# A retrieval feed-forward layer: one of five dense token blocks keeps its dense first product, but fetches its chosen values and gathers rows of the second table

## The chip, the cores and the metric

The kernel runs on one core of one Trainium2 chip. The metric is the device time of one execution in microseconds (us). TensorE is called PE, VectorE DVE, ScalarE ACT and GpSimd POOL, as in the profile; SP is the engine that issues most of the ordinary DMAs, PEld the weight loads of PE. Each engine takes its instructions in the order in which the program lists them.

## The reference

One layer with 1024 tokens of width 1024: a mixer (a gated linear recurrence and a state-space group, both behind one input projection), then a feed-forward layer with product-key retrieval over 128 x 128 = 16384 experts, and a last norm. The change is in the retrieval layer:

```python
q = (xb @ wq).reshape(TOK_BLOCK, 8, 256)            # 8 heads
s1 = einsum('thd,kd->thk', q[..., :128], k1)        # 128 keys each
s2 = einsum('thd,kd->thk', q[..., 128:], k2)
v1, i1 = top_k(s1, 16); v2, i2 = top_k(s2, 16)
sc, cidx = top_k(all sums v1 + v2, 16)              # 16 experts a head
e = i1[cidx // 16] * 128 + i2[cidx % 16]
g = softmax(sc)
act = gelu(einsum('thkd,td->thk', u_tab[e], xb))    # first product
out = einsum('thk,thkd->td', g * act, v_tab[e])     # second product
```

So each token picks 8 x 16 = 128 experts. An expert is one row of u_tab (the first table) and one row of v_tab (the second), 1024 float32 numbers, 4 KB each.

## The kernel before, in words

The tokens lie in 8 blocks of 128. After the mixer (`front`) the retrieval layer (`peer`, L848) does the blocks in two ways.

**Gathered blocks** (the last NG = 3). `topk` (L982) finds the experts, `topk_gather` (L1067) writes their indices. `gather` (L1150) fetches, for k = 0 to 127, the k-th chosen row of the first table for all 128 tokens with one indirect DMA on POOL (`fetch`, L1130: 128 rows of 4 KB, 512 KB) and multiplies it with the tokens on DVE (tile `jkb`), which gives one column of `act`. After the gelu and the product with the gate weights `gw`, `act` is transposed on PE, and 128 indirect DMAs fetch rows of the second table, which PE sums up four at a time (tile `pgb`). A ring of ROWS = 7 buffers (`row`) holds the rows, with six fetches ahead. `finish` (L1197) does the last norm and stores the block.

**Dense blocks** (the first ND = 5, 640 tokens). The first product is made for all 16384 experts. For each of 128 slices j (`first`, L1217): load and split a 512 KB slice of the first table (tiles `ur`, `uh`, `ul`: float32 numbers as a sum of two shorter ones), 48 matmuls in two halves of 320 columns (tile `ap`), gelu on ACT. `build_g` (L1080) spreads a block's 128 gate weights per token over a matrix of all experts by products of one-hots (tiles `ohA`, `ohB`, `gp`, `gs`), which goes to DRAM as `G_d`. In `dense` (L1296) come 32 chunks of JC = 4 slices j: load the gate matrix (`gt`), multiply the first product by it (`hr` or `ha`), split it (`hh`, `hl`), load and split four slices of the second table (`vr`, `vh`, `vl`), and multiply: for each block 24 matmuls of 512 columns into a PSUM tile (`vp`, two buffers), which DVE adds to the block's result (`h`, L1363).

**What sets the order.** `Merge` (L62) is a planner: the parts are generators, and at each `yield` the one with the lowest clock goes on. The clocks come from costs that `Timed` (L121) charges for each compute instruction; a DMA is only charged where `mg.dma` and `mg.at` say so, and `Timed` hands DMA starts through without a charge (L128). The result is a fixed order of instructions for each engine. The stages are:

1. The norm and the queries of the gathered blocks, then (L1274) the queries of the dense blocks, the top-k of the gathered blocks and the start of the gathers.
2. The build stage (L1284): for each dense block the top-k and its gate matrix (`build`, L1278), and beside it first products made ahead (`ahead`, L1238), stored to DRAM as `A_d`. The order of j takes one slice of each chunk in turn, NA = 112 at most; 84 get done. Gathers go on, no closer than `pace` = 5.0 us of the planner's clock.
3. The dense stage (L1381): the 32 chunks. Of the 128 slices, 84 come back from `A_d`, the 44 late ones are made between the chunks, spread over all of them. Here the gathers are let through by `share`: a budget of DMA bytes that grows with PE's planned time (`step`, L1375) minus the bytes that the dense work loads.

SP issues the loads and the stores of `G_d` and `A_d`, POOL the indirect DMAs. Matmuls and most DVE and ACT instructions go through a helper, so that they all bear L146; in the profile they are told apart by their tiles.

Of the kernel before, what the change touches and what calls it, by code (L numbers as in the profile page):

```python
# [18 lines left out]
P = 128  # L19
D = 1024  # L20
# [815 lines left out]
ND = 5  # L836
NG = 8 - ND
TD = ND * P
HALF = TD // 2
TG = NG * P  # L840
JC = 4
NA = 112
# [5 lines left out]
def peer(tc, a, cst, pools, h, ss, mg):  # L848


    nc = tc.nc
# [4 lines left out]
    gblocks, dblocks = list(range(ND, 8)), list(range(ND))  # L856
# [4 lines left out]
    H_d = dr.tile([NG, P, D], F32, name="H_d")  # L861
# [4 lines left out]
    xDh = pc.tile([P, 8, TD], F32R, name="xDh")  # L866
    xDl = pc.tile([P, 8, TD], F32R, name="xDl")
    idx = [pc.tile([P, P], I32, name=f"idx{b}") for b in range(NG)]
    idxT = [pc.tile([P, P], I32, name=f"idxT{b}") for b in range(NG)]
    gw = [pc.tile([P, P], F32, name=f"gw{b}") for b in range(NG)]  # L870
# [4 lines left out]
    V.tensor_copy(i16, iota[:, 0:16])  # L875

# [24 lines left out]
    def norm2():  # L901
        for blocks in (gblocks, dblocks):
# [3 lines left out]
            for b in blocks:  # L906
# [69 lines left out]
    rows = pools.open("rows", bufs=ROWS)  # L976
    gp = pools.open("gp", bufs=2)
# [89 lines left out]
    def topk_gather(b):  # L1067
        i1, i2, g = yield from topk(b)
        n = b - ND
        V.scalar_tensor_tensor(i1, i1, 128.0, i2, ALU.mult, ALU.add)  # L1070
        V.tensor_copy(idx[n], i1)
# [77 lines left out]

    def gather(n):  # L1150
        xg = gp.tile([P, D], F32, name="xg", tag="xg", bufs=1)
        nc.sync.dma_start(xg, X_d[n])
        act = gp.tile([P, P], F32, name="act", tag="act", bufs=1)
        k = 0
        for ub in stream(a["peer_u"], [idx[n][:, k:k + 1] for k in range(P)]):
            yield gate()
            jk = gp.tile([P, D], BF, name="jkb", tag="jkb", bufs=1)
            V.tensor_tensor_reduce(jk, ub, xg, 1.0, 0.0, ALU.mult, ALU.add, act[:, k:k + 1])
            k += 1
            mg.units += 1  # L1160
        S.activation(act, act, AF.Gelu_apprx_tanh)
        yield
# [67 lines left out]

    order = [c * JC + jj for jj in range(JC) for c in range(P // JC)]
# [34 lines left out]
    def topks():  # L1266
        for n in range(NG):
            yield from topk_gather(ND + n)

    def dense_query():  # L1270
        yield from query(pqb, dblocks, xDh, xDl)
# [19 lines left out]
    pv = pools.open("pv", "right", bufs=4)  # L1291
    phh = pools.open("phh", "right", bufs=4)
    pgg = pools.open("pgg", "right", bufs=1)
    nch = P // JC

    def dense():  # L1296
        late = [[] for _ in range(nch + 1)]
        order[made[0]:] = sorted(order[made[0]:], key=lambda j: j // JC)
        for j in order[made[0]:]:
            late[j // JC].append(j)  # L1300
        ha = {}

        def products(js):
            for j in js:
                fetch_u()
# [158 lines left out]
```

## Time and profile before

| | |
|---|---|
| median of 3 runs | 3043.96 us (3030.63 to 3053.36) |
| profiled execution, its own time | 3037.66 us |
| its span | 3035.9 us |
| mean granted TensorE clock | 0.961 of full speed |
| HBM read, written | 664.75 MB, 85.20 MB |
| DMA, mean over the span | 248 GB/s |
| mixer and first norm | 0 to about 400 us |
| queries, first top-k | about 400 to 720 us |
| build stage | about 720 to 1593 us |
| dense stage | about 1593 to 3036 us |

How the lines are read. A row of a stretch gives from:to, its length, the busy time of each engine with the number of instructions, the granted TensorE clock (1.0 is full speed), the mean busy share of the 16 DMA engines, and GB/s. A row of a group gives line, engine, operation, out<-in, shapes and count, then busy time and mean duration in ns, then the idle time of the engine ahead of them and what ended it. Busy time of a group is a union: overlapping instructions count once, which is why count times mean duration of matmuls is more than the busy time. Float32 matmuls that are not split show up as two records. A few per cent of the matmul records are missing. A row of the waits gives who waited for whom, the sum in us, how often, and the longest. A row of the chain gives start, length and what ran there. A DMA row gives the count, the size of one and the median us from issue to landing.

### The profile page before, as it was taken

The numbers are of one execution on the slowest core, as the hardware profiler recorded it, in microseconds if no ns is written. First come the engines' busy times: TensorE is split into PE (matmuls) and PEld (weight loads), VectorE is DVE, ScalarE is ACT, GpSimd is POOL, SyncE is SP. The second block draws the span as 40 slices with busy tenths as digits, with TensorE's granted clock in tenths as the row PEclk, the third lists the DMA queues.
The fourth block names the chain that finished last, engine by engine and source line by source line (L and its number), as shares of the span: only waits on it lengthen the run. The fifth ranks groups of instructions, "written<-read, shape, count | busy, mean of one in ns | idle before, by whom it ended". The sixth has DMA issues, their size and how long they took to land.

```text
span 3035.9 us, 43516 instructions
## 1 busy us (share of the span) xinstructions
PE 2783.9 (92%) x16261; PEld 2352.3 (77%) x16261; DVE 2029.8 (67%) x4241; ACT 1155.0 (38%) x2273; POOL 955.2 (31%) x778
## 2 busy tenths in 40 slices
PE   6887999987999999999989999999999999999998
PEld 6765878877899988888877777676768788767675
DVE  7786452999999994332349999644547999643434
ACT  5355433321684958584852222211222212121212
POOL 0000000132526012222244555343435556343431
PEclk9988999988999999999999999999999999999999
DMA  4112144565989658888899889877878899787774
GB/s 156 28 26 100 42 138 128 181 223 197 309 305 350 217 193 289 277 277 290 274 327 343 328 325 322 304 251 285 323 293 305 319 342 344 268 303 260 257 275 160
DMA packets 298532, 754.01 MB, mean 248 GB/s; under 512 B 28368, under 2 KB 125840, under 8 KB 293200
## 3 DMA queue, kind: packets, MB, share of 16 engines
q0 software_dynamic: 110592, 402.70, 37.3%
q1 hardware_dynamic: 180992, 337.33, 31.8%
q10 hardware_dynamic: 6736, 11.19, 1.1%
q8 instruction: 128, 2.10, 0.3%
q14 instruction: 84, 0.69, 0.1%
HBM read 664.75 MB, written 85.20 MB: 247 GB/s over the span
## 4 chain that ended last, share of the span: by engine, by line
PE 36%; DVE 11%; DMA 9%; issue 7%; ACT 1%; POOL 1%; DVEq 0%; POOLq 0%; ACTq 0%
PE vp L146 14%; PE ap L146 13%; PE pgb L146 6%; DVE jkb L146 5%; PE gp L146 3%; DMA row<-in_peer_v_dram,idxT 3%; DMA ur<-in_uT_dram 2%; DVE h L146 2%; DVE vl L146 2%; DMA gt<-G_d 2%; DMA hr<-A_d 1%; DVE hl L146 1%; DMA A_d<-aa 1%; DVE hr L146 1%; POOL row L1132 1%
## 5 line engine op out<-in xcount | busy, mean ns | idle before, releaser
L1132 POOL DMA_INDIRECT row<-in_peer_u_dram,idx x384 | 525.2, 1368 | 772.8 <-DVE act L146 335.8
L1132 POOL DMA_INDIRECT row<-in_peer_v_dram,idxT x384 | 426.2, 1110 | 921.7 <-PE pgb L146 794.8
L146 PE MATMUL ap<-xDl,uh 128*128 128x320 f32 x2048 | 657.0, 321 | 25.9 <-ACT ha L146 21.4
L146 PE MATMUL ap<-xDh,ul 128*128 128x320 f32 x2048 | 644.4, 315 | 6.1 <-DVE ul L146 6.1
L146 PE MATMUL ap<-xDh,uh 128*128 128x320 f32 x2048 | 642.0, 314 | 0.0
L146 PE MATMUL vp<-vl,hh 128*128 128x512 f32 x1280 | 510.0, 400 | 39.6 <-DVE vl L146 29.4
L146 PE MATMUL vp<-vh,hl 128*128 128x512 f32 x1280 | 504.4, 394 | 0.7 <-DVE hl L146 0.7
L146 PE MATMUL vp<-vh,hh 128*128 128x512 f32 x1280 | 502.5, 393 | 0.0
L146 DVE CUSTOM_DVE_ANT_0 jkb<-row,xg 128x1024 bf16<-128x1024 f32 x384 | 468.4, 1220 | 10.9 <-DMA row<-in_peer_u_dram,idx 8.1
L146 PEld LDWEIGHTS ap<-xDl,uh 128*128 128x128 f32 x2048 | 392.7, 192 | 67.5 <-issue 29.3
L146 PEld LDWEIGHTS ap<-xDh,ul 128*128 128x128 f32 x2048 | 392.7, 192 | 9.1 <-DVE ul L146 7.4
L146 PEld LDWEIGHTS ap<-xDh,uh 128*128 128x128 f32 x2048 | 392.4, 192 | 1.3
L146 PEld LDWEIGHTS vp<-vl,hh 128*128 128x128 f32 x1280 | 242.0, 190 | 134.1 <-issue 27.5
L146 DVE TENSOR_TENSOR h<-h,vp 128x1024 f32<-128x1024 f32 x160 | 194.6, 1216 | 190.7 <-PE vp L146 190.7
L146 ACT ACTIVATE hh<-ha 128x640 fp32r<-128x640 f32 x44 | 32.3, 735 | 659.4 <-PE vp L146 654.8
L146 PEld LDWEIGHTS vp<-vh,hh 128*128 128x128 f32 x1280 | 242.5, 189 | 51.7
L146 PEld LDWEIGHTS vp<-vh,hl 128*128 128x128 f32 x1280 | 242.8, 190 | 50.9 <-DVE hl L146 2.7
L146 DVE TENSOR_TENSOR ul<-ur,uh 128x1024 fp32r<-128x1024 f32 x128 | 156.5, 1222 | 137.1 <-ACT uh L146 137.0
L146 PE MATMUL pgb<-row,W 128*32 128x512 f32 x1536 | 204.0, 608 | 24.9 <-DMA row<-in_peer_v_dram,idxT 24.9
L146 DVE TENSOR_TENSOR ohA<-iota,kt 128x512 f32<-128x512 f32 x160 | 110.2, 689 | 166.5 <-PE gp L146 166.3
L146 PE MATMUL gp<-ohB,ohA 128*128 128x128 f32 x1280 | 185.2, 282 | 22.7 <-DVE ohB L146 12.9
L146 ACT ACTIVATE ohB<-ohB,kt 128x128 f32<-128x128 f32 x480 | 203.9, 489 | 0.0
(422 smaller groups left out, 4194.6 us busy)
## 6 DMA issues: line engine op xcount, KB each, us to landing
ur<-in_uT_dram SPq DMA_DIRECT2D x128, 512.0 KB, 5.8
vr<-in_peer_v_dram SPq DMA_DIRECT2D x128, 512.0 KB, 6.8
G_d<-gs SPq DMA_DIRECT2D x20, 2048.0 KB, 11.7
gt<-G_d SPq DMA_DIRECT2D x32, 1280.0 KB, 8.6
A_d<-aa SPq DMA_DIRECT2D x84, 320.0 KB, 5.8
hr<-A_d SPq DMA_DIRECT2D x84, 320.0 KB, 7.1
wqr<-in_wq_dram SPq DMA_DIRECT2D x32, 512.0 KB, 4.0
S_d<-sc SPq DMA_DIRECT2D x64, 128.0 KB, 4.0
```

The costliest lines, as they stand in the source:

```text
L146: return fn(*args, **kw)
L1132: G.indirect_dma_start(out=r, out_offset=None, in_=table, in_offset=bass.IndirectOffsetOnAxis(ap=col, axis=0))
```

## The change

ND becomes 4, and a third kind of block comes in: NE = 1 block whose first product is still made densely, with the four others (NU = ND + NE = 5 blocks, TU = 640 columns), and whose second product is gathered.

- `first` and the queries work on the same 640 columns as before. After the first product of slice j, the 512 columns of the dense blocks go on as before, and the 128 columns of the fifth block are stored to DRAM in `E_d` (`chosen_only`, 64 KB a slice). After the last slice the planner's flag "U" is set.
- `values` fetches the fifth block's chosen values: 128 indirect DMAs on POOL, each of one number for each of 128 tokens, from `E_d` into the columns of `act`. Nothing in it moves the planner's clock. Then `act` is multiplied by `gw`, transposed, and rows of the second table are gathered as for the other gathered blocks.
- The gathers take blocks 6 to 8 first and the fifth last, after "U".
- Only four gate matrices are built. The fifth block's top-k comes after them, ahead of flag "g".
- First products are made ahead in the order of j (no NA), until "g" and then to the end of a chunk. The dense stage begins with the chunks whose first product is late and ends with those made ahead; each chunk is prepared while the second product of the one before is done. The parts of `dense` are written anew for that, and a tile `gt` has its buffer in the pool `phh`.
- The pace of the gathers in the build stage goes from 5.0 to 2.4 us, and the planned costs of a first and a second product are set to 7.0 and 2.7 us (6.5 and 2.6 before).

The diff, cut to its core:

```diff
-ND = 5
-NG = 8 - ND
+ND = 4
+NE = 1
+NU = ND + NE
+NG = 8 - NU
+NR = NE + NG
 TD = ND * P
-HALF = TD // 2
+TE = NE * P
+TU = NU * P
+HALF = TU // 2
 TG = NG * P
 JC = 4
-NA = 112
...
-    gblocks, dblocks = list(range(ND, 8)), list(range(ND))
+    gblocks, ublocks, dblocks = list(range(NU, 8)), list(range(NU)), list(range(ND))
...
-    H_d = dr.tile([NG, P, D], F32, name="H_d")
+    H_d = dr.tile([NR, P, D], F32, name="H_d")
+    E_d = dr.tile([P, P, TE], F32, name="E_d")
...
+    rows = pools.open("rows", bufs=ROWS)
+    gp = pools.open("gp", bufs=2)
+    pxu = pools.open("pxu")
+    xDh = pxu.tile([P, 8, TU], F32R, name="xDh")
+    xDl = pxu.tile([P, 8, TU], F32R, name="xDl")
...
-        for blocks in (gblocks, dblocks):
+        for blocks in (gblocks, ublocks):
...
-                    nc.sync.dma_start(X_d[b - ND], xn)
                     nc.sync.dma_start(H_d[b - ND], h[b])
-                    dh, dl, t0 = xGh, xGl, (b - ND) * P
+                if b >= NU:
+                    nc.sync.dma_start(X_d[b - NU], xn)
+                    dh, dl, t0 = xGh, xGl, (b - NU) * P
...
+        if n < NE:
+            at = pk.tile([P, P], F32, name="at", tag="rf")
+            V.scalar_tensor_tensor(at, i2, 128.0, i1, ALU.mult, ALU.add)
+            V.tensor_scalar(at, at, float(TE), tok[:, n:n + 1], ALU.mult, ALU.add)
+            V.tensor_copy(idx[n], at)
...
+        if n >= NE:
+            V.tensor_copy(idx[n], i1)
...
+    def values(n):
+        act = gp.tile([P, P], F32, name="ace", tag="ace")
+        flat = E_d.rearrange("j i t -> (j i t)").unsqueeze(1)
+        for k in range(P):
+            G.indirect_dma_start(out=act[:, k:k + 1], out_offset=None, in_=flat,
+                                 in_offset=bass.IndirectOffsetOnAxis(ap=idx[n][:, k:k + 1], axis=0))
+            if k % 8 == 7:
+                yield
+        return act
     def gather(n):
-        xg = gp.tile([P, D], F32, name="xg", tag="xg", bufs=1)
-        nc.sync.dma_start(xg, X_d[n])
-        act = gp.tile([P, P], F32, name="act", tag="act", bufs=1)
-        k = 0
-        for ub in stream(a["peer_u"], [idx[n][:, k:k + 1] for k in range(P)]):
-            yield gate()
-            jk = gp.tile([P, D], BF, name="jkb", tag="jkb", bufs=1)
-            V.tensor_tensor_reduce(jk, ub, xg, 1.0, 0.0, ALU.mult, ALU.add, act[:, k:k + 1])
-            k += 1
-            mg.units += 1
-        S.activation(act, act, AF.Gelu_apprx_tanh)
-        yield
+        if n < NE:
+            act = yield from values(n)
+        else:
+            xg = gp.tile([P, D], F32, name="xg", tag="xg", bufs=1)
...
+            S.activation(act, act, AF.Gelu_apprx_tanh)
+            yield
         V.tensor_tensor(act, act, gw[n], ALU.mult)
...
     def fetch_u(end=P):
         if len(nextu) < 2 and made[0] + len(nextu) < end:
-            nextu.append(load_split(pu, a["uT"][order[made[0] + len(nextu)]], [8, P], "u"))
+            nextu.append(load_split(pu, a["uT"][made[0] + len(nextu)], [8, P], "u"))
+    def chosen_only(j, t):
+        nc.sync.dma_start(E_d[j], t[:, TD:])
+        mg.dma(TE // 2)
+        if j == P - 1:
+            mg.flag("U")
     def ahead():
         fetch_u()
         yield
         while nextu:
-            t = pk2.tile([P, TD], F32, name="aa", tag="aa")
-            j = order[made[0]]
+            t = pk2.tile([P, TU], F32, name="aa", tag="aa")
+            j = made[0]
             for n, _ in enumerate(first(t, nextu[0])):
-                if n == 0 and "g" not in mg.flags:
-                    fetch_u(NA)
-                yield
-            nc.sync.dma_start(A_d[j], t)
-            mg.dma(320)
+                if n == 0:
+                    fetch_u(P if "g" not in mg.flags else JC * -(-(j + 1) // JC))
+                yield
+            nc.sync.dma_start(A_d[j], t[:, :TD])
+            mg.dma(TD // 2)
+            chosen_only(j, t)
             made[0] += 1
             nextu.pop(0)
...
-        for n in range(NG):
+        for n in list(range(NE, NR)) + list(range(NE)):
             if f"g{n}" not in mg.flags:
                 yield f"g{n}"
+            if n < NE and "U" not in mg.flags:
+                yield "U"
             yield from gather(n)
...
+        for n in range(NE, NR):
             yield from topk_gather(ND + n)
...
+        yield from query(pqb, ublocks, xDh, xDl)
...
         for b in dblocks:
             yield from build_g(b)
+        for n in range(NE):
+            yield from topk_gather(ND + n)
         mg.flag("g")
-    pace[0] = 5.0
+    pace[0] = 2.4
...
+    pv = pools.open("pv", "right", bufs=JC)
+    phh = pools.open("phh", "right", bufs=JC)
+    nch, nah = P // JC, made[0] // JC
...
+        def prepare(c):
+            gt = phh.tile([P, TD, JC], F32, name="gt", tag="gt", bufs=1)
             nc.sync.dma_start(gt, G_d[c])
-            mg.dma(1280)
+            mg.dma(TD * JC // 2)
             for j in range(c * JC, c * JC + JC):
+                if c < nah:
+                    hr = phh.tile([P, TD], F32, name="hr", tag="ha", bufs=4)
+                    nc.sync.dma_start(hr, A_d[j])
+                    mg.at(mg.dma(TD // 2))
+                else:
+                    hr = phh.tile([P, TU], F32, name="ha", tag="ha", bufs=4)
+                    fetch_u()
+                    for n, _ in enumerate(first(hr, nextu[0])):
+                        if n % 2 == 0:
+                            step(3.5, 512 / 2)
+                        if n == 0:
+                            fetch_u()
+                        yield
+                    chosen_only(j, hr)
+                    made[0] += 1
+                    nextu.pop(0)
+                yield
+                hr = hr[:, :TD]
+                V.tensor_tensor(hr, hr, gt[:, :, j % JC], ALU.mult)
+                yield
+                x = phh.tile([P, TD], F32R, name="hh", tag="hh")
+                lo = phh.tile([P, TD], F32R, name="hl", tag="hl")
+                split_to(x, lo, hr)
+                yield
+                done.append((x, lo) + load_split(pv, a["v"][:, j], [D], "v"))
+                yield
+        order = list(range(nah, nch)) + list(range(nah))
+        done = []
+        yield from prepare(order[0])
+        for n, c in enumerate(order):
+            ts, done = done, []
+            side = prepare(order[n + 1]) if n + 1 < nch else iter(())
+            hh, hl, vh, vl = zip(*ts)
...
+                        PE.matmul(p_[:, i], hh[jj][:, bs], vl[jj][:, ns], start=(jj == 0), stop=False)
+                        PE.matmul(p_[:, i], hl[jj][:, bs], vh[jj][:, ns], start=False, stop=False)
+                        PE.matmul(p_[:, i], hh[jj][:, bs], vh[jj][:, ns], start=False, stop=(jj == JC - 1))
+                    step(2.7, (JC * (512 + TD // 2 * (2 if c < nah else 1))) / (2 * ND))
+                    next(side, None)
                     yield
+                    next(side, None)
                 V.tensor_tensor(acc[b], acc[b], p_.rearrange("p a b -> p (a b)"), ALU.add)
-                if c == nch - 1:
+                if n == nch - 1:
                     finish(b, acc[b])
                 yield
+            yield from side
...
-    left = 2 * NG * P - units0
-    late = P - made[0]
-    pe, kb = late * 6.5 + nch * 2.6 * 2 * ND, P * 832 + late * 512 + made[0] * 320
+    left = (2 * NG + NE) * P - units0
+    pe = (P - made[0]) * 7.0 + nch * ND * 2 * 2.7
+    kb = P * (512 + TD // 2) + (P - made[0]) * 512 + made[0] * TD // 2
```

`load_split` (L1208), `first`, `fetch`, `stream`, `finish` and `step` are called as they were. Left out above are the lines of the old order (`order`, `late`, `products`, `weigh`) that `prepare` replaces, the closing of pools, and lines of the old `gather` that only move to the right.

More of the change, by code (lines that the diff above doesn't have):

```diff
@@ L865, in peer @@
     pc = pools.open("pc")
[L866 to L870, printed above, removed]
+    idx = [pc.tile([P, P], I32, name=f"idx{n}") for n in range(NR)]
+    idxT = [pc.tile([P, P], I32, name=f"idxT{n}") for n in range(NR)]
+    gw = [pc.tile([P, P], F32, name=f"gw{n}") for n in range(NR)]
+    tok = pc.tile([P, NE], F32, name="tok")
+    G.iota(tok, pattern=[[P, NE]], base=0, channel_multiplier=1, allow_small_or_imprecise_dtypes=True)
     eye = pc.tile([P, 32, 32], BF, name="eye")
@@ L1228, in first @@
             yield
-    order = [c * JC + jj for jj in range(JC) for c in range(P // JC)]
     made, nextu = [0], []
@@ L1266, in topks @@
     def topks():
-        for n in range(NG):
+        for n in range(NE, NR):
             yield from topk_gather(ND + n)
     def dense_query():
-        yield from query(pqb, dblocks, xDh, xDl)
+        yield from query(pqb, ublocks, xDh, xDl)
         mg.flag("q")
@@ L1382, in peer @@
     mg.run([])
-    pools.close("pgg", "phh", "pv", "ppv", "ppa", "ppg", "pu", "gp", "rows", "pc", "acc", "dram")
+    pools.close("phh", "pv", "ppv", "ppa", "ppg", "pu", "pxu", "gp", "rows", "pc", "acc", "dram")
 def body(tc, a):
```

68 lines of the change are left out of this document (10 added, 58 removed).

## The prediction

> **What bounds the kernel now.** I read the page first (busy shares, then the groups), then the busy time by stretch of the span, then the waits and the chain. The three stretches from 541 us on are: the query and first top-k, the build stage (the gate matrix G, with first products made ahead), and the dense stage.
>
> ```profile
> PE 2783.9 (92%) x16261; PEld 2352.3 (77%) x16261; DVE 2029.8 (67%) x4241; ACT 1155.0 (38%) x2273; POOL 955.2 (31%) x778
> q0 software_dynamic: 110592, 402.70, 37.3%
> q1 hardware_dynamic: 180992, 337.33, 31.8%
> ```
> ```profile
> 541.00:720.00 179.00, 148.74 (x953) 143.81 (x952) 171.11 (x714) 42.50 (x91) 51.34 (x43) 0.91 0.63 209
> 720.00:1593.00 873.00, 825.90 (x5840) 764.93 (x5840) 573.65 (x1755) 573.07 (x1394) 275.10 (x233) 0.97 0.82 278
> 1593.00:3036.00 1443.00, 1356.94 (x6930) 1063.03 (x6930) 955.94 (x1159) 302.03 (x412) 624.89 (x492) 0.98 0.81 295
> ```
> In the last two rows (length, then busy PE, PEld, DVE, ACT, POOL with their counts, then clock, DMA share, GB/s) PE is busy 2182.8 of 2316 us, 133 us idle, and the 16 DMA engines are busy 0.82 and 0.81 of it. So TensorE carries the time, and the transfers stand close behind it. What a product costs is its spacing, since durations overlap:
>
> ```profile
> 2143.22 11.15 PE vp L146 x48
> 2154.37 1.85 PE pgb L146 x16
> 2156.22 11.15 PE vp L146 x48
> 2169.22 7.23 PE ap L146 x48
> ```
> A second-product matmul (vp) takes 11.15/48 = 0.232 us. The 48 first-product matmuls (ap) of one j take 7.23 us. Sixteen pgb records, four gathered rows of the second table, take 1.85 us, 0.46 us a row. The groups give the counts:
>
> ```profile
> L146 PE MATMUL vp<-vl,hh 128*128 128x512 f32 x1280 | 510.0, 400 | 39.6 <-DVE vl L146 29.4
> L146 PE MATMUL pgb<-row,W 128*32 128x512 f32 x1536 | 204.0, 608 | 24.9 <-DMA row<-in_peer_v_dram,idxT 24.9
> L146 PE MATMUL gp<-ohB,ohA 128*128 128x128 f32 x1280 | 185.2, 282 | 22.7 <-DVE ohB L146 12.9
> ```
>
> **The change, part by part.** *Second product.* Each of three groups has 1280 matmuls for five blocks. Four blocks leave 3072 of 3840: 768 x 0.232 = 178 us off PE.
>
> *Gate matrix.* Four builds for five: a fifth of gp's 185.2 us, 37 us off PE. The one-hots, copies and G_d stores go with it and are off the path (DVE and ACT are busy 0.66 of that stage). Top-k still runs for all eight blocks; the fifth moves behind the last build, with three small DVE operations more: nothing.
>
> *First product and query.* Still 640 columns in two halves of 320, so still 128 x 7.23 us and the same queries. Only their stage moves. How many are made ahead follows from the order written by the planner, which four builds and one more top-k now bound:
>
> ```profile
> L146 DVE COPY kt<-gt x5: 549/553/559, 783.7 to 1440.9; 128x384 f32<-128x384 f32 x5
> ```
> ```profile
> 720.00:1441.00 721.00, 62.39 (x144) 0.97 0.81 273
> ```
> The first row dates the fifth build's start, which comes after four builds and five top-k: 1440.9 us. The second counts the ACT results of first products up to there, 144, two for each j: 72 made, a multiple of four. So 56 fall late instead of 44: 12 x 7.23 = 87 us leave the build stage and come back in the dense stage.
>
> *Rows of the second table for the fifth block.* 128 more: 128 x 0.46 = 59 us onto PE. With the three above, PE's work falls by 178 + 37 - 59 = 156 us, to 2027 us.
>
> *The pace (5.0 to 2.4).* Between no more fetches in the build stage and 5/2.4 times as many. I take about 80 more, since the planner also charges a row's own work. They come off the dense stage, so this moves transfers, not their sum.
>
> *Transfers.* A row fetch occupies the engines 37.3% x 3036 / 768 = 1.47 us; 128 more are 189 us. The ordinary queue pays 31.8% x 3036 / 337.33 = 2.86 us per MB.
>
> ```profile
> G_d<-gs SPq DMA_DIRECT2D x20, 2048.0 KB, 11.7
> gt<-G_d SPq DMA_DIRECT2D x32, 1280.0 KB, 8.6
> A_d<-aa SPq DMA_DIRECT2D x84, 320.0 KB, 5.8
> hr<-A_d SPq DMA_DIRECT2D x84, 320.0 KB, 7.1
> ```
> A fifth of G_d both ways is 16.8 MB less. A_d goes from 84 x 320 KB to 72 x 256 KB both ways, 17.3 MB less. E_d adds 128 stores of 64 KB, 8.4 MB, and H_d half a MB: 25 MB less, 72 us. Net +117 us on 0.82 x 873 + 0.81 x 1443 = 1885 us: 2002 us of full DMA. The fully hidden end is the best stretch of the trace, the dearer end the dense stage of before; these rows stand between them:
>
> ```profile
> 2403.00:2603.00 200.00, 190.16 (x950) 165.30 (x949) 191.91 (x256) 43.22 (x60) 122.92 (x86) 0.98 0.93 341
> 2803.00:3003.00 200.00, 187.59 (x1007) 133.46 (x1005) 76.85 (x75) 35.80 (x49) 65.20 (x61) 0.97 0.66 240
> ```
> At 0.93 with u rows in flight PE still does 190 of 200 us. I take a mean of 0.91, a little under that row: 2002/0.91 = 2200 us, of which 2027 are PE's, so 173 us idle, 40 more than before. At 0.95 it would be 2107 us (80 idle, 53 fewer); at 0.85, 2355 us (195 more).
>
> *E_d stores on SP's queue.* In the late chunks each store waits for a gelu on ACT and stands ahead of the vr load of the same j, whose split then holds ACT. Before, PE lost little to such chains:
>
> ```profile
> PE vp L146 <- DVE vl L146: 29.4, 21, 4.1
> PE ap L146 <- ACT ha L146: 21.4, 3, 15.2
> ```
> A store can't gain anything; twice the two sums, 102 us, is the other end. I leave it inside the 40 us. In the build stage the stores follow A_d's, which wait for the same gelu: nothing.
>
> *The dense stage turned round* (chunks with late products first) has the same work; U is complete with 19 of 32 second products left. What DVE does for a chunk stands in these rows:
>
> ```profile
> L146 DVE TENSOR_TENSOR h<-h,vp 128x1024 f32<-128x1024 f32 x160 | 194.6, 1216 | 190.7 <-PE vp L146 190.7
> L146 DVE TENSOR_TENSOR vl<-vr,vh 128x1024 fp32r<-128x1024 f32 x128 | 156.1, 1220 | 14.2 <-ACT vh L146 12.2
> L146 DVE TENSOR_TENSOR hr<-hr,gt 128x640 f32<-128x640 f32 x84 | 109.6, 1308 | 69.5 <-DMA hr<-A_d 61.0 <-issue 8.5
> L146 DVE TENSOR_TENSOR hl<-hr,hh 128x640 fp32r<-128x640 f32 x84 | 68.8, 819 | 0.0
> ```
> With 512 columns in place of 640 the last two become 1.05 and 0.66 us. An ahead chunk asks 4 x (1.22 + 1.22 + 1.05 + 0.66) = 16.6 us of DVE against 96 x 0.232 = 22.3 us of PE: room, as long as no u rows fall there. Its transfers are 4.2 MB (12 us) and some nine rows (13 us), 25 us, just under PE's 22.3 + 9 x 0.46 = 26.4 us: cover, with little to spare. The opened pools, tok and the H_d and X_d stores cost nothing that a later step waits for.
>
> *The values.* 128 indirect DMAs of 128 single numbers on POOL. The planner charges nothing for an indirect DMA, so all 128 are written out at one point, and right behind them on DVE stands the multiply of act by gw, which waits for the last. DVE works in order: behind it are vl, hr, hl and the additions h that free the PSUM tiles of vp; on PE the transposes of act stand in line too, and on POOL the fifth block's first row fetches. Price on POOL, from fetches that waited for nothing:
>
> ```profile
> 1566.13 0.94 POOL L1132 DMA_INDIRECT row<-in_peer_u_dram,idx  x1 [3.98 <-DMA out_dram<-hb]
> 1567.37 0.94 POOL L1132 DMA_INDIRECT row<-in_peer_u_dram,idx  x1 [0.30 <-issue]
> 1568.62 1.33 POOL L1132 DMA_INDIRECT row<-in_peer_u_dram,idx  x1 [0.30 <-issue]
> ```
> The first two start 1.24 us apart. In the stretch with DVE 96% busy (2403 to 2603) a fetch takes 122.92/86 = 1.43 us, in that with DVE 38% busy 65.20/61 = 1.07 us. With DVE waiting I take 0.94 + 0.30: 128 x 1.24 = 159 us. The Trainium skill ("SBUF — State Buffer", Who interferes with whom) says that a VectorE instruction with two SBUF inputs contends with a GpSimd one that reads SBUF; the two stretches agree in direction, 1.43 against 1.07 us. By that rule a stalled DVE leaves 159 us; without it the busy figure, 1.43 + 0.30, would make 221 us, 62 us more.
>
> POOL starts ahead of DVE. At the end of the first gathered block:
>
> ```profile
> 1534.82 1.10 POOL L1132 DMA_INDIRECT row<-in_peer_v_dram,idxT  x1 [6.95 <-PE pgb L146]
> ```
> ```profile
> 1550.00 1.22 DVE L146 TENSOR_TENSOR hb<-hb,pgb 128x1024 f32<-128x1024 f32 x1 [3.11 <-PE pgb L146]
> 1556.92 1.28 DVE L146 SCALAR_TENSOR_TENSOR hb<-hb,st,nf 128x1024 f32<-128x1024 f32 x1
> ```
> The last row fetch ended at 1535.9, DVE was through with the block at 1558.2: 22 us ahead. PE covers at most two PSUM tiles more, 2 x 24 x 0.232 = 11 us. The last value lands some 6.5 us after issue, as rows do:
>
> ```profile
> row<-in_peer_v_dram,idxT POOLq DMA_INDIRECT x384, 6.5
> ```
> So PE stands for 159 + 6.5 - 22 - 11 = 133 us. Bounds: nothing, if the multiply sits behind other work; 195 us at the busy figure.
>
> **Sum**, against the profiled execution's 3037.66 us (span 3035.9; the median of the runs is 3043.96, 0.2% above): - 178 - 37 + 59 + 40 + 133 = +17, so 3055 us, no change that a measurement here can tell (about 1%, 3014 to 3074).
>
> **The rivals.**
> 1. *The values cost PE nothing* (the multiply is late enough, or other chunks are prepared ahead). For: POOL is busy 31%. Against: DVE is in order, and nothing in the planner delays the multiply. 3055 - 133 = 2922 us, faster.
> 2. *The transfers pack as tightly as in the best stretch*, share 0.95: 3055 - 93 = 2962 us, faster. Against: with u rows, DVE and DMA are at 0.96 and 0.93 together already.
> 3. *The transfers bind* (the other side): row fetches of late chunks, now with u, v, gt and E_d beside them, hold PE; share 0.85 gives 3055 + 155 = 3210 us, 0.88 (2275 us) 3130 us. It decides below a share of 0.90, where 2002/0.90 is 24 us more and the 1% is crossed.
> 4. *The values are dearer*: 1.73 us each gives 3117 us, slower. The Trainium skill ("DMA: Bandwidth & Descriptors", Anatomy of one DMA) gives a fixed cost of about 2.0 us per DMA, mostly completion; rows of this trace are issued 1.24 us apart and land 6.5 us later, so here it overlaps. Were it paid in turn, as a chain of 128 landings 2 us apart, an estimate from that page would be 256 us of fetches and 3152 us in all.
>
> **How the numbers follow.** Forecast 0.32; values free 0.16; tight packing 0.14; transfers binding 0.19; dearer values 0.19. Faster 0.30, same 0.32, slower 0.38. Leaving out the values-free case and the far end of the binding one, the range is 2940 to 3165 us; the forecast's own is 3014 to 3074.
>
> **What would show it.** Right: 3072 vp and 2048 pgb records; 72 A_d stores; one hole of 130 to 160 us on PE and DVE in the second half of the dense stage while POOL issues 128 DMAs 1.24 us apart; G_d's stores ending near 1440 us; DMA share around 0.9 outside the hole. Wrong: no such hole (then 2922 us), a hole over 190 us, or PE idle in the late chunks on row fetches by far more than 40 us.

## The result

The changed kernel takes 3331.27 us (median of 4 runs, 3327.39 to 3343.09) against 3046.93 us of the kernel before on the same chip: a ratio of 1.095 (95% interval 1.090 to 1.100). The forecast was 3055 us, and 3165 us the upper end of its range. The profiled execution took 3343.09 us, its span is 3341.3 us, its mean granted clock 0.926 (before 0.961).

### The profile page after: what moved, and what is told of

Same layout as the page of the kernel before. It is cut to its first block, busy times and chain, and to the rows that moved or that the text cites. A ratio compares the mean times of both kernels' runs of the same rounds, so it can differ in the third digit from the quotient of the medians.

```text
span 3341.3 us, 42855 instructions
## 1 busy us (share of the span) xinstructions
PE 2924.9 (88%) x15748; PEld 2227.2 (67%) x15748; DVE 1933.2 (58%) x4167; ACT 1066.9 (32%) x2049; POOL 1233.0 (37%) x1035
## 3 DMA queue, kind: packets, MB, share of 16 engines
q1 hardware_dynamic: 182112, 316.89, 27.8%
## 4 chain that ended last, share of the span: by engine, by line
PE 51%; DVE 14%; DMA 11%; issue 8%; POOL 5%; ACT 3%; SPq 0%; POOLq 0%; DVEq 0%; ACTq 0%
PE vp L146 16%; PE ap L146 15%; PE pgb L146 11%; DMA row<-in_peer_u_dram,idx 4%; PE qp L146 3%; DMA row<-in_peer_v_dram,idxT 3%; POOL row L1150 3%; DVE jkb L146 3%; PE wop L146 2%; POOL ace L1173 2%; PE gp L146 2%; DVE ix L146 2%; DVE oh L146 1%; ACT ohB L146 1%; DVE v L146 1%
## 5 line engine op out<-in xcount | busy, mean ns | idle before, releaser
L1150 POOL DMA_INDIRECT row<-in_peer_v_dram,idxT x512 | 548.1, 1071 | 1075.3 <-PE pgb L146 923.0
L146 PE MATMUL vp<-vl,hh 128*128 128x512 f32 x1024 | 434.5, 424 | 153.5 <-DVE vl L146 109.9
L146 PE MATMUL pgb<-row,W 128*32 128x512 f32 x2048 | 473.1, 608 | 31.3 <-DMA row<-in_peer_v_dram,idxT 29.1
L146 PE MATMUL vp<-vh,hl 128*128 128x512 f32 x1024 | 422.5, 413 | 0.0
L146 PE MATMUL vp<-vh,hh 128*128 128x512 f32 x1024 | 422.4, 413 | 0.0
L146 PEld LDWEIGHTS vp<-vl,hh 128*128 128x128 f32 x1024 | 200.0, 195 | 309.3 <-DVE vl L146 131.0
L146 ACT ACTIVATE hh<-hr 128x512 fp32r<-128x512 f32 x80 | 49.8, 623 | 776.1 <-PE vp L146 672.3
L146 PEld LDWEIGHTS vp<-vh,hh 128*128 128x128 f32 x1024 | 200.2, 196 | 105.6 <-issue 66.2
L146 PEld LDWEIGHTS pgb<-row,W 128*32 128x32 f32 x2048 | 81.3, 109 | 238.5 <-issue 175.5
L146 DVE TENSOR_TENSOR vl<-vr,vh 128x1024 fp32r<-128x1024 f32 x128 | 156.5, 1223 | 60.0 <-ACT vh L146 58.7
```

Source lines behind the costliest of these rows:

```text
L146: return fn(*args, **kw)
L1150: G.indirect_dma_start(out=r, out_offset=None, in_=table, in_offset=bass.IndirectOffsetOnAxis(ap=col, axis=0))
```

## The profile after

First the page's line of the engines, and the groups of the two second products and of the gate matrix:

```profile
PE 2924.9 (88%) x15748; PEld 2227.2 (67%) x15748; DVE 1933.2 (58%) x4167; ACT 1066.9 (32%) x2049; POOL 1233.0 (37%) x1035
L146 PE MATMUL vp<-vl,hh 128*128 128x512 f32 x1024 | 434.5, 424 | 153.5 <-DVE vl L146 109.9
L146 PE MATMUL pgb<-row,W 128*32 128x512 f32 x2048 | 473.1, 608 | 31.3 <-DMA row<-in_peer_v_dram,idxT 29.1
L146 PE MATMUL gp<-ohB,ohA 128*128 128x128 f32 x1024 | 152.3, 285 | 46.9 <-ACT gs L146 29.1
```

The counts are those forecast: 3 x 1024 = 3072 vp and 2048 pgb records, and gp fell by 33 us (37 were forecast). But pgb went from 204.0 to 473.1 us, where 59 us more were forecast, and PE's busy time rose by 141 us, where 156 us less work was forecast.

The stores of E_d (line, queue, count, then durations in ns and the first and last start) date the stages:

```profile
L1270 SPq DMA_DIRECT2D E_d<-aa x80: 422/425/4758, 733.0 to 1574.8; - x80
L1270 SPq DMA_DIRECT2D E_d<-ha x48: 319/323/577, 1587.7 to 2240.2; - x48
L1173 POOL DMA_INDIRECT ace<-E_d,idx x128: 940/952/1993, 2292.8 to 3003.2; - x128
```

80 slices are made ahead and 48 late: 12 late chunks, from about 1590 to 2240 us, and then 20 chunks made ahead. The last row is the values: not one block of 160 us but spread over 710 us. The stretches, as for the kernel before:

```profile
720.00:1590.00 870.00, 783.51 (x5426) 721.10 (x5426) 627.28 (x1843) 493.37 (x1164) 386.87 (x303) 0.95 0.89 309
1590.00:2240.00 650.00, 636.85 (x3700) 543.51 (x3702) 299.75 (x338) 155.62 (x233) 179.56 (x147) 0.99 0.62 220
2240.00:3341.00 1101.00, 897.59 (x3154) 434.43 (x3148) 509.77 (x672) 137.69 (x187) 610.46 (x533) 0.89 0.78 277
```

The build stage ends where it ended before. The late chunks run at PE's pace (637 of 650 us) with the transfers only 0.62 busy. The whole loss is in the last row: 20 chunks take 1101 us, 55 us each, where the forecast had 22.3 us of vp and nine rows, 26.4 us, for each. POOL's count of the second row is 147, all of them row fetches; of the 533 of the third, 128 are values and 405 rows: 20 for each chunk made ahead, not nine. What waited from 2240 us on (who for whom, us, times, longest):

```profile
ACT hh L146 <- PE vp L146: 672.3, 18, 64.6
POOL row L1150 <- PE pgb L146: 315.1, 68, 7.6
PE vp L146 <- DVE vl L146: 109.9, 26, 10.4
```

ACT stood 672 us until PE had ended a second product, to be able to write the next chunk's `hh`; PE in turn stood 110 us until that chunk's `vl` was there. All 110 us of that lie between 2311 and 2700 us, so the 20 chunks fall into two parts, here with a stretch of each:

```profile
2500.00:2700.00 200.00, 113.71 (x390) 72.72 (x389) 128.93 (x179) 25.26 (x34) 154.34 (x127) 0.72 0.80 272
2700.00:2900.00 200.00, 199.96 (x699) 79.88 (x699) 69.01 (x74) 24.92 (x32) 84.75 (x83) 1.00 0.81 297
```

In the first part most of the values go out among rows, 109 of 128 by 2700 us. POOL is nearly full there: 154.34 us and 127 gaps of 0.30 us are 192 of 200 us. PE is busy for 114 us, at a granted clock of 0.72, and behind a pause it is also slow for a while. After a wait of 5.05 us, vp matmuls start 0.43 us apart from 2431 to 2436 us, and only then 0.23 us apart again. By the spacing of its vp rows this is some 30 us from 2311 to 2700 us (an estimate). In the second part PE is never idle, at a clock of 1.00, and a chunk still takes about 51 us: pgb is busy for 103 us with 324 records, about twenty fours, which at 1.85 us each would take 37. So the lower clock goes with the pauses and is not what makes the second part long. PE's own rows (start, length, out<-in, records) show what became of four gathered rows:

```profile
2857.07 1.04 PE L146 MATMUL pgb<-row,W 128*32 128x512 f32 x2
2858.05 0.50 PE L146 MATMUL vp<-vh,hl 128*128 128x512 f32 x1
...
2858.94 1.04 PE L146 MATMUL pgb<-row,W 128*32 128x512 f32 x2
2859.92 0.50 PE L146 MATMUL vp<-vh,hl 128*128 128x512 f32 x1
...
2861.73 1.04 PE L146 MATMUL pgb<-row,W 128*32 128x512 f32 x2
2862.71 0.50 PE L146 MATMUL vp<-vh,hh 128*128 128x512 f32 x1
...
2864.53 1.90 PE L146 MATMUL pgb<-row,W 128*32 128x512 f32 x10
```

The eight matmuls (16 records) of four rows mostly stood together before and took 1.85 us. Here three single ones lie between matmuls of vp, then five together. A single one takes 0.98 us from its start to the next vp, the five 1.83 us: 3 x 0.98 + 1.83 = 4.8 us in all. In the program's order for PE 64 of all 128 fours are split like that; in the trace, where some records are missing, 187 single ones can be counted, which makes at least 62 fours. The kernel writes the eight of a four down in one loop (L1217), so the issue order on PE is not the order in which the planner wrote it down. It looks as if instructions that are ready first were listed first; no run tests that.

Three suspects come out of this: rows held back into the chunks made ahead, the turn-around of one chunk's buffers, split fours. The values are a fourth.

## Experiments: one cause at a time

The times below stand beside 3043 to 3055 us of the kernel before on the same chips. Where no interval is given it is one run. The kernel before itself differs by up to 13 us between these chips, so a smaller difference between single runs tells nothing.

**Fours together, and gathers not held back.** `together` lists the other seven matmuls of a four directly behind the first; `bias` takes away the handicap with which the planner starts a gather after a dense step; `tog_bias` does both.

```diff
-            for c in range(2):
-                for j in range(4):
-                    PE.matmul(pga[32 * j:32 * j + 32, c], ...)
+            with tc.issue_after(mm(0, 3).ins):
+                for c in range(2):
+                    for j in range(4 if c else 3):
+                        mm(c, j)
```
```diff
     step(0.0, 0.0)
+    for th in mg.ths:
+        th["bias"] = -1000.0
     mg.add([(0.0, dense())])
```

> The eight products of each four gathered rows stand together on PE, as most did before the change. In the changed kernel 64 of 128 such fours are split into 1, 1, 1 and 5 among vp, and one of them then costs PE about 5.5 us instead of 2.05. Split fours as the cause: 64 x 3.5 = 224 us off PE, of which transfers (share 0.76 over the last 610 us) leave at least 110: 3110 to 3220 us. The values on POOL as the cause, or the planner holding rows back in the late chunks: no change, 3310 to 3350 us.

> The gathers' handicap in the planner goes from +2 to -1000 in the dense stage, so that they are let through as far as the byte budget allows (30 rows a late chunk instead of 16). The planner as the cause: the last block's u rows leave the ahead chunks, where DVE has 5.7 us of room a chunk, and DMA (0.53 to 0.67 in the late chunks) fills up: 150 us less, 3180 us. Split fours as the cause: about 35 fours stay split in place of 64, 60 to 100 us less. Values as the cause: they no longer meet u rows, 90 us less.

> Both edits: fours together and the gathers let through up to the budget. If split fours and the planner's order carry the loss, together they give back most of it: about 3050 us, the time that the sum of the prediction gave (3000 to 3100). If the values carry it, 3200 us or more is left, with a hole on PE while POOL issues them.

Measured: 3229.69, 3202.64, and 3197.73 us for both (4 runs; ratio to before 1.048, 1.044 to 1.052). Each mend is worth 102 and 129 us by itself, but both together only 134: something else holds. `together` came out 10 us above the range for split fours and `bias` 22 us above the figure for the planner; `tog_bias` missed the range of 3000 to 3100 by 98 us. The gathers did move; the row fetches of `bias` (length, POOL busy with its count, clock, DMA share, GB/s):

```profile
1590.00:2240.00 650.00, 352.42 (x280) 0.96 0.86 312
2240.00:3201.00 961.00, 292.92 (x267) 0.92 0.68 247
```

280 rows beside the first product where the changed kernel had 147, and 267 behind it where it had 405.

**The values.** `novalues` leaves the 128 fetches out of the changed kernel, `tog_bias_noval` out of `tog_bias`; the fifth block's numbers are then not the chosen ones.

```diff
-        for k in range(P):
-            G.indirect_dma_start(out=act[:, k:k + 1], out_offset=None, in_=flat, ...)
+        nc.sync.dma_start(act, E_d[0])
```

> Leaves out the 128 value fetches: the fifth block's act is loaded with one plain DMA instead. The values as the cause: from 2300 to 2670 us POOL issues about 110 values between the u rows of the last gathered block at 1.58 us each, 174 us; the second products that were done meanwhile (about 4 chunks, 85 us) come later, so 90 us less, 3240 us. A full hole as predicted would give 133 us less. Split fours or the planner as the cause: no change, 3310 to 3350 us.

> The same version (3198) without the 128 fetches of values (one plain load in their place, so the fifth block's numbers are not the chosen ones). Against the changed kernel alone leaving them out gave 103 us. If the values crowd POOL in the ahead part also here, it falls by 80 to 130 us, to about 3090; if the buffers' turn-around binds that part, the gap closes only by 0 to 40 us.

Measured: 3228.83 (102 us less) and 3086.77 (111 us less).

**The turned order alone.** Five dense blocks as before and none of the new kind, in the changed kernel's order of the dense stage.

```diff
-ND = 4
-NE = 1
+ND = 5
+NE = 0
```

> Five dense and three gathered blocks as before (no block of the new kind), but the changed kernel's dense stage: late chunks first, then the chunks made ahead, pace 2.4, the same preparation. If the turned order is what costs (a chunk made ahead can be prepared only as fast as the one before it gives its buffers back, with no first products between), the chunks made ahead take well over their 5 x 24 x 0.232 = 27.8 us, about 36, and the whole takes 3120 to 3200 us. If only the fifth block's new way costs (values, rows), it is at 3044, within 30 us.

Measured: 3234.59 us, 179 us over the kernel before on that chip (3055.39, one run; on the other chips it takes 3043 to 3047 us). So nearly two thirds of the loss of 284 us come with an edit that the forecast priced at nothing. The pace of 2.4 us and the new planned costs come along with it. ACT's rows show where it goes (start, length, what ended the wait ahead in brackets):

```profile
2709.62 0.74 ACT L146 ACTIVATE hh<-hr 128x640 fp32r<-128x640 f32 x1 [31.71 <-PE vp L146]
2711.22 0.72 ACT L146 ACTIVATE hh<-hr 128x640 fp32r<-128x640 f32 x1
2712.80 0.72 ACT L146 ACTIVATE hh<-hr 128x640 fp32r<-128x640 f32 x1
2714.36 0.72 ACT L146 ACTIVATE hh<-hr 128x640 fp32r<-128x640 f32 x1
2717.72 1.06 ACT L146 ACTIVATE vh<-vr 128x1024 fp32r<-128x1024 f32 x1 [2.64 <-DMA vr<-in_peer_v_dram]
2750.50 0.74 ACT L146 ACTIVATE hh<-hr 128x640 fp32r<-128x640 f32 x1 [31.71 <-PE vp L146]
```

`hh`, `hl`, `vh` and `vl` have four buffers each: one chunk. The next chunk's four can be split only when the last vp of this one is done, and its first vp needs all four. From one such start to the next it is 40.9 us where the five vp take 27.8: 13 us of turn-around. They are not all lost, since PE does two fours there, 3.7 us if whole. Of PE's time from 2238 us on, 67 us are waits for `vl` and 56 us waits for rows, and pgb takes 152.5 us for 634 records, 79 us more than whole fours would (some 30 of 96 are split here): 202 us, some 9 us a chunk (an estimate). In the kernel before, the late first products of every chunk (7.23 us each on PE) lay in that gap; turned round, 23 chunks in a row (92 slices, made ahead here) have none.

**A second set of buffers.** In every second chunk made ahead, `hh` and `hl` lie in the tile `xDh` of the dense tokens, `vh` in `xDl`, and `vl` in the tiles of the first table's split slices, all idle by then.

```diff
+                e = c < nah and c % 2
+                if e:
+                    x, lo = xDh[:, i, :TD], xDh[:, JC + i, :TD]
...
+                    vh = xDl.rearrange("p a b -> p (a b)")[:, D * i:D * i + D]
+                    vl = pu.tile([P, D], F32R, tag=("uh", "ul")[i % 2], name="vl")
```

It was put on the changed kernel alone (`double_only`), with one mend (`double_tog`, `double_bias`), with both (`double`), and on the turned order with five dense blocks and both mends (`turned_double`).

> The version with fours kept together and gathers not held back (3198), and in the chunks made ahead every second chunk has its hh, hl, vh, vl in tiles that are idle there (the dense tokens and the split slices of the first table), so that a chunk can be prepared before the one ahead of it has ended its second product. If the turn-around of those buffers holds the last 885 us (20 chunks of 44 us against 22.3 of PE and 12 rows of 0.46), ACT's 443 us of waiting for vp go and the time falls to 2950 to 3030 us, under the kernel before. If rows and values bind there (POOL, six fetches in flight), it stays at 3198, within 40 us.

> The turned order with five dense and three gathered blocks (3235), fours kept together, gathers not held back, and the second set of buffers in the chunks made ahead. If the 13 us a chunk between the last second product of one and the first of the next were the price of turning, 23 such chunks give back 200 to 300 us: 2940 to 3040. If the price lies elsewhere (rows, clock), it stays above 3150.

> The changed kernel (3331) with the second set of buffers alone; fours still split and gathers still held back. On the mended version the second set gave 143 us. If the split fours (5.5 us of PE in place of 1.9) and the turn-around are separate prices, about the same goes: 3170 to 3220. If the split rows only lay in the time of the turn-around, less than 60 us goes: above 3270.

> The changed kernel (3331) with the second set of buffers and the fours kept together, gathers still held back. The fours alone gave 102 us, the second set alone 8 to 20. If these two hide each other (PE fills the turn-around with split fours, or is held by the one or the other), both together give much more than their sum, about 200 us: 3100 to 3150. If they only add, 3210 to 3225.

> The changed kernel (3331) with the second set of buffers and the gathers not held back, fours still split where the planner's code lets them. Gathers not held back gave 129 us alone, and with them few rows are left that can be split, so most of the 143 us of the second set should show here: 3070 to 3110. If the split of the rows left still hides the second set, it stays above 3170.

Measured: `double` 3054.28, `turned_double` 3042.32, `double_only` 3323.14, `double_tog` 3266.88, `double_bias` 3108.63 us. The same stretch of `turned` and of `turned_double` shows what the three mends do to the turned order:

```profile
2700.00:2900.00 200.00, 182.62 (x783) 119.83 (x782) 96.71 (x92) 32.60 (x40) 56.14 (x44) 0.94 0.62 234
2700.00:2900.00 200.00, 198.84 (x971) 144.51 (x970) 115.03 (x110) 39.19 (x48) 62.14 (x54) 1.00 0.80 288
```

In the first PE does 783 records and no other engine, nor the transfers, are near full; in the second PE is full with 971. A chunk there takes 31.4 us instead of about 40, and 9 us in 23 chunks are 207 us, close to the 192 us between the two runs. The second set was not put on the turned order without the other two mends.

With the gathers not held back the second set gives 94 us (3202.64 to 3108.63), with the fours together as well 143 us (3197.73 to 3054.28). Without that it gives 8 us, less than the chips differ. `double` came out 24 us above its range, `double_bias` at the edge of it, and `double_tog` above both of its forecasts. In `double_tog` 403 rows are left for the chunks made ahead, and POOL is full for a part of them, so that there a second set of buffers can't help:

```profile
2400.00:2600.00 200.00, 124.67 (x396) 93.90 (x394) 149.64 (x208) 28.14 (x34) 161.29 (x128) 0.77 0.80 273
```

161.29 us of POOL and 128 gaps of 0.30 us are 199.7 of 200 us. From 2600 us on POOL is less busy (96 of 200 us from 2800 to 3000), and what holds PE there is not shown. Why `double_tog` is 37 us slower than `together`, one run each, stays open.

**Late first products spread again.** On `tog_bias`, two late slices in each of chunks 0 to 23, in natural order.

```diff
+    order = list(range(JC * 24, P)) + [c * JC + jj for jj in range(JC) for c in range(24)]
...
-            nextu.append(load_split(pu, a["uT"][made[0] + len(nextu)], [8, P], "u"))
+            nextu.append(load_split(pu, a["uT"][order[made[0] + len(nextu)]], [8, P], "u"))
...
-        order = list(range(nah, nch)) + list(range(nah))
-        for n, c in enumerate(order):
+        for n in range(nch):
+            c = n
```

> The same version (3198) with the late first products spread two to a chunk over chunks 0 to 23, in natural order, and only chunks 24 to 31 without any. If bare chunks cost about 44 - 28 = 16 us each, 12 fewer of them give back 190 us, but now U is complete only some 240 us before the end and 128 values of 1.24 us and 128 rows of 1.3 us (325 us on POOL) lie behind it, so about 100 us come back: about 3100. If bare chunks don't cost, the late U alone makes it 3250 or more.

Measured: 3161.35 us, 36 less: the cover came back, and the late U took most of it. Here the forecast hole stands in the trace, first as waits, then as stretches:

```profile
DVE ace L146 <- DMA ace<-E_d,idx: 101.5, 1, 101.5
PE pga L146 <- DVE ace L146: 101.1, 1, 101.1
```
```profile
2699.00:2767.00 68.00, 63.60 (x253) 48.96 (x252) 39.57 (x39) 12.19 (x16) 53.13 (x49) 0.92 0.47 157
2767.00:2868.00 101.00, 0.09 (x1) 0.00 (x0) 0.20 (x1) 0.00 (x0) 75.22 (x80) 0.52 0.02 0
```

All 128 values went out in one run from 2699.2 to 2866.3 us, 1.3 us each. PE had work for the first 68 us and then stood 101 us for the multiply of `ace` by `gw`.

**Where the values lie.** `double_charge` makes the planner count a value as 0.9 of a row. The `double_weave` versions issue two values behind each row fetch of the last gathered block after U, and count them as 0.9, 0.15 and 0.35 of a row.

```diff
         for k in range(P):
+            yield gate()
             G.indirect_dma_start(out=act[:, k:k + 1], ...)
+            mg.units += 0.9
```
```diff
             yield gate()
             mg.units += 1
+            for _ in range(2 if n == NR - 1 and "U" in mg.flags else 0):
+                if len(vk) <= P:
+                    value(0)
```

> The version with the second set of buffers (3054), and the planner is told of the values: each counts as 0.9 of a row in the budget that lets the gathers through, so more rows go into the late chunks (their DMA share was 0.78 to 0.86 there) and no fours are listed on PE while the 128 values are fetched. Leaving the values out of the version with one set gave 111 us, so if crowding on POOL and fours listed too early are what they cost, 80 to 160 us go: 2900 to 2970, under the kernel before. If 128 values cost their 159 us of POOL wherever they lie, it stays at 3054, within 30 us.

> The version with the second set of buffers (3054) without the 128 fetches of values (one plain load in their place, so the fifth block's numbers are not the chosen ones): the floor for any placing of them. If the values still cost what they did with one set (111 us), 2945. If the buffers had made room for them, above 3020.

> The version with the second set of buffers (3054), with two values issued on POOL behind each row fetch of the last gathered block after U (so no long run of values), and the budget raised from U on by 0.9 of a row for each value. If it is the long runs of values that stop PE (30 us at the multiply with the second set, about 160 us of slow PE when all 128 came in one run), and a value between rows costs only its POOL time, which is free there, it comes near the 2960 of the version without values: 2930 to 2990, under the kernel before. If 128 values cost about 95 us wherever they are, it stays at 3054, within 25 us.

> As double_weave (3051), but a value counts only 0.15 of a row in the budget, so the planner spreads the 204 rows left at U evenly, about 10 to 11 to a chunk, instead of 6 to a chunk beside the values and 17 after them. In double_weave the DMA share was 0.69 to 0.79 beside the values and up to 0.96 after them. If that imbalance is what the values still cost, about 7 chunks of 35 us (POOL: 10 fetches of 1.4 us and 17 values of 1.25 us) and 13 of 31 us (DMA) give 650 us after U and 2960 to 2990 us in all. If the values cost about 95 us wherever they are, 3050, within 20 us.

> The same with 0.35 of a row for each value: between the two, 2975 to 3020 if the balance of rows decides; 3050, within 20 us, if the values' price does not depend on it.

Measured: `double_charge` 3157.33 us (6 runs; ratio 1.038, 1.036 to 1.041), `double_noval` 2959.63 us, `double_weave` 3050.98 us (10 runs; 1.002, 0.999 to 1.005), `double_weave_15` 3045.43 us (10 runs; 1.001, 0.998 to 1.003), `double_weave_35` 3029.45 us (6 runs; 0.994, 0.991 to 0.996). The first was a clear miss, told below. `double_weave` and `double_weave_15` missed the forecasts by which a better place would give 2930 to 2990 us, and `double_weave_35` fell between its two. The woven ones have no run of values and no hole, and still come only 3 to 25 us below the one run of `double`: among rows the values cost 70 to 95 us in each of these places. Beside them POOL is full (`double_weave_15`, then the same stretch of `double_noval`):

```profile
2400.00:2500.00 100.00, 69.70 (x316) 45.72 (x318) 39.98 (x42) 18.29 (x24) 77.75 (x74) 0.86 0.72 234
```
```profile
2400.00:2500.00 100.00, 93.67 (x469) 61.84 (x468) 51.49 (x55) 18.29 (x24) 46.79 (x43) 0.97 0.94 352
```

77.75 us and 74 gaps of 0.30 us make 100 us of POOL, and PE did 316 matmul records in place of 469. `double_weave_35` is the best version with all of the work: 0.6% under the kernel before on its chip.

## Why the prediction was wrong, by its steps

One chain of runs adds up: 3331 (changed), 3203 (gathers not held back, -129), 3109 (second set, -94), 3054 (fours together, -54), 2960 (no values, -95). In another order the parts differ, since each covers some of the others: the fours alone gave 102 us, the second set alone 8. All but the first of these times are single runs.

- *"The dense stage turned round ... has the same work"*, priced at nothing: **the step that failed.** The work is the same, but the late first products had covered the turn-around of buffers that hold one chunk. `turned` shows 179 us for the turned order with its pace and planned costs, and `turned_double`, which keeps all of these and adds the three mends, is at the kernel before (3042.32 against 3043.91): the order costs by what it uncovers and earns nothing. How the 179 us divide between the buffers, the rows held back and the split fours is not shown, and in the changed kernel the second set of buffers pays only behind the other mends. The step looked at sums of engine time per chunk (16.6 us of DVE beside 22.3 of PE) and not at which buffer lets the next chunk begin. The row that should have warned was quoted in the forecast: even with cover, vp waited 29.4 us for `vl`.
- *"Some nine rows"* for a chunk made ahead: it was 20. The build stage got 303 row fetches where it had 233, 70 more (80 were forecast), but the late chunks, with a DMA share of 0.62, took only 147. That rows would be shared out by the budget was assumed, not read from the order. By the chain this is 129 us. The transfers did not bind there, against the third rival.
- *59 us of PE for 128 more rows* at 0.46 us a row: holds only for fours that stay together. In `double_noval` pgb takes 263.8 us, 60 more than before; in the changed kernel 269 more.
- *The values, 133 us, as one hole*: the size was near (102, 111 and 95 us by leaving them out), the form was not. That the order written down is the order issued was the wrong premise: values came among the last gathered block's u rows. The hole of the forecast appears in `spread24`, with 101 us, since PE had 68 us of other work and not 33. The rival that they cost nothing is false: beside them POOL is full (`double_weave_15`).
- *The price of one value*, 0.94 + 0.30 us: right in `spread24`, where DVE mostly stood, with a median of 0.944 us and a mean of about 1.00. Among u rows, in the changed kernel, the median is 0.952 us but the mean 1.23 (157.3 us busy for 128): a part of them takes far longer. The Trainium skill ("SBUF — State Buffer", Who interferes with whom) lets a VectorE instruction with two SBUF inputs contend with a GpSimd one that reads SBUF; the two means agree in direction. The last value landed 2.4 us after its issue in `spread24`, not 6.5.
- *A chain of 128 landings*, estimated at 256 us from the Trainium skill's fixed cost of about 2.0 us per DMA ("DMA: Bandwidth & Descriptors", Anatomy of one DMA): did not come. 128 of them were issued in 167 us, so that cost overlaps here too.
- *-178, -37, and the transfers*: right as far as they can be told apart. The forecast without the values was 2922 us; `double_noval` is at 2960, with a DMA share of 0.92 to 0.95 from 2400 to 2800 us while PE is busy for 94 to 100 of each 100 us, so the transfers can pack more tightly than the 0.91 assumed. That `double` is at 3054 where 3055 was forecast is partly luck, 38 us too low in the sum and 38 too high for the values; but it tells that the forecast described this kernel with the three mends in it, which it had taken for granted.
- *72 stores of A_d, the build's end near 1440 us*: 80, and the last one-hot of the gate matrix starts at 1452 us, the last store of G_d at 1477 us.

## What to carry to other kernels

Before a reordering is priced at nothing, ask for each step what lay between it and the next, and how many buffers let the next one begin: work that is "moved" takes its cover with it, and a first estimate of the price is the turn-around, less what still fills it, times the number of steps left bare (here 9 us in 23 chunks). Here the sum of engine times per stage came true, partly by luck, for a kernel with its buffers and issue order mended; for the kernel as written, read the issue order and count the rows per stage. And where three limits lie close together, a mend that is worth next to nothing alone (8 us) may be worth a hundred microseconds behind another (94 and 143).

## What was not expected of the hardware

A single 32-column pgb matmul between vp matmuls takes 0.98 us of PE (changed kernel), eight together 1.85 us (kernel before).

In `double_charge` the 128 values ran alone on POOL from 2497 to 2664 us, the multiply came late (2730.6 us), and no wait for them shows on PE. Yet from 2530 to 2690 us PE was busy for 37 of 160 us, and in long parts of it issued one matmul in 2.8 us:

```profile
2530.00:2690.00 160.00, 37.08 (x73) 19.78 (x72) 15.63 (x16) 6.30 (x8) 109.00 (x111) 0.52 0.17 50
```
```profile
2605.88 0.59 PE L146 MATMUL vp<-vl,xDh 128*128 128x512 f32 x1 [2.21 <-issue]
2608.68 0.59 PE L146 MATMUL vp<-xDl,xDh 128*128 128x512 f32 x1 [2.21 <-issue]
2611.48 0.59 PE L146 MATMUL vp<-xDl,xDh 128*128 128x512 f32 x1 [2.21 <-issue]
```

No semaphore explains it ("issue"). The instruction queue q8 moved no packet between 2515 and 2670 us, where it else moves one in some 30 us; but whether that is cause or effect the trace does not tell, and in `spread24` PE ran on for 68 us beside the first values, with one packet in each 30 us. All 6 runs of `double_charge` are about as long, so it is no accident of one execution. What holds PE there was not found. The 123 us that it is idle in this stretch are more than the 103 us by which that version is over `double`.
